# A lookahead of three halves in the first five steps, two transposes two steps later, and three fewer products of zeros

## The chip, the cores and the metric

The kernel runs on one core of a Trainium2 chip. The metric is device time in microseconds (us); lower is better. A time is the median of several executions; the profile is one execution, recorded by the hardware profiler, whose own time is given beside its span. Engines are named as in the profile: PE is TensorE (PEld its weight loads), DVE is VectorE, ACT is ScalarE, POOL is GpSimd and SP is SyncE, which issues most DMAs.

## The reference, cut to what matters

One layer on 256 tokens of width 1024, all in float32: a mixer of two attentions, then a gated feed-forward net with a short convolution, each followed by a residual and a layer norm.

```python
mod = silu(c) @ w_ada + b_ada                      # six rows of 1024: shifts, scales, gates
h = x * (1 + sc1) + sh1
mq, mk, mv, rq, rk, rv, rg, g_a, g_r = split(h @ w_in)
y_a = softmax attention of 8 heads (rotary_half(mq), rotary_half(mk), mv), causal
y_r = retention of 4 heads (retnet_rotate(rq), retnet_rotate(rk), rv); y_r = silu(rg) * head_norm(y_r)
merged = sigmoid(g_a) * (y_a @ w_proj_moba) + sigmoid(g_r) * (y_r @ w_proj_ret)
x = layer_norm(1.189 * x + g1 * (merged @ w_out))
h = x * (1 + sc2) + sh2                            # then the feed-forward net and the second norm
```

`rotary_half` turns each half of a head's q or k against the other: `x1*cos - x2*sin`, `x2*cos + x1*sin`. That is the "rotation" below.

## The kernel before, in words

**Split products.** Every float32 product is made of products of rounded parts. A weight half (a 128x1024 tile, "half" for half of a 1 MB load) is split into `whi`, a rounded copy made by ScalarE (line 1197), and `wlo`, the rest, made by VectorE (line 1211). `mm3` (lines 90 to 93) then makes three TensorE products: high by high, high by low, low by high.

**First phase, up to about 59 us.** It makes the modulation rows and the first columns of `h @ w_in` while their weights arrive (lines 143 to 322). It begins with products of zeros: `fill(n)` (line 160) puts n products of a 128x128 and a 128x512 tile of zeros on TensorE, `PRE` = 4 of them before the eight transposes of line 182 and `POST` = 22 behind them. The first real products are those of line 241, whose high parts come from lines 202 and 221.

**The main loop.** From there on a list `steps` holds one entry per weight half (lines 1246 to 1269 run it). Steps 0 to 3 make rk (load `winB`), 4 to 9 rv (`winV`), 10 to 17 rg, 18 to 33 the gates (`winGr`), 34 to 45 the two projections, and so on. A step of this part is 12 products of 128x512, or from step 18 on 24 of 128x256. Before its products a step prepares (splits) halves ahead: `prep_to(max(need) + 1 + LOOKAHEAD)` with `LOOKAHEAD` = 6, so step s has the halves up to s+6 split in the engines' queues ahead of its own products. There are 8 buffers for split halves and 4 for raw loads; a raw load is issued when the second half of an earlier one has been split. ScalarE's copy of one half more is queued ahead (`ahead`, line 1208). Behind some splits a chained reduction of the modulation rows runs on VectorE (line 174, "ada" in the names).

**The mixers ride along.** `mixers()` (line 955) is a generator that the loop advances three times per step: before the splits, between the splits and the products, and behind the products. Its first part rotates q and k of the two token tiles with eight VectorE operations, at most three per step (lines 919 to 928: two partner products, the product with cos, the sum). `ROT_AT` = 3 says how many steps it rotates before the transposes: behind the products of step 3 `rot_T` transposes q and k of token tile 0 on TensorE (line 934, eight transposes into banks 4 and 5) and ScalarE copies them out (line 936); behind step 4 the same for token tile 1. From the next step on, `i` counts the steps of the attention: `scores` every second step (line 995 on TensorE, line 1001 on VectorE), Exp in the next (line 1027 on ScalarE), its reciprocal (line 1031, VectorE), the scaling (line 1023, ScalarE), four steps behind the scores three transposes per head into bank 5 (line 1038, TensorE) and their copy (line 1040, ScalarE), and the weighted sum of a pair of heads into bank 6 (`attend`, line 1014). In steps 5 to 8 of this count VectorE also rotates q and k of the retention; later come its transposes and the retention itself.

**What is set by the step number and not by `i`.** The sums of rv (line 497) follow steps 6 and 9. The silu of rg follows the products of steps 13 and 17 by one step: it stands in steps 14 and 18, a Sigmoid on ScalarE (line 507) and a product on VectorE (line 508). ScalarE's functions come in tables; where the next function is not in the loaded one, an `ACT_TABLE_LOAD` stands ahead of it.

Engines run their queues in order, so the place of an operation in the program is its place in the queue. The loop's lines that the change touches:

```python
late = LN1_AT < s < LN1_AT + 8
if not late:
    prep_to(max(need) + 1 + (LOOKAHEAD if s < LN1_AT - 1 else HL_BUFS))
run_sides()
```

Of the kernel before, what the change touches and what calls it, by code (L numbers as in the profile page):

```python
# [20 lines left out]
LOOKAHEAD = 6  # L21
RAW_BUFS = 4
HL_BUFS = 8
NG = 4
ROT_AT, RV_AT, RG_AT, LN1_AT = 3, 10, 18, 50


CONST_AT = 1
T0_AT, XN, PRIME = 4, 256, 3
W0, W1, W2 = (4, 5), (6,), (7,)  # L30
PRE, POST = 4, 22


def mixer_ffn(tc, a, out):
    nc = tc.nc
    pe, act, dve, sp = nc.tensor, nc.scalar, nc.vector, nc.sync
    cst = tc.tile_pool(name="cst", bufs=1)
    pools = [cst, tc.tile_pool(name="wts", bufs=1), tc.tile_pool(name="big", bufs=1),
             tc.tile_pool(name="tmp", bufs=2),
             tc.tile_pool(name="ps", bufs=1, space=bass.MemoryType.PSUM),  # L40
             tc.tile_pool(name="dram", bufs=1, space=bass.MemoryType.DRAM)]
    with tc.manual_schedule():
        with pools[0] as cst, pools[1] as wts, pools[2] as big, pools[3] as tmp, pools[4] as ps, \
                pools[5] as dram:
            _body(nc, a, out, pe, act, dve, sp, cst, wts, big, tmp, ps, dram)


def _body(nc, a, out, pe, act, dve, sp, cst, wts, big, tmp, ps, dram):
# [424 lines left out]
    def run_waiting(early):  # L473
        for e in waiting:
            if e[0] <= S["main"] and (not early or e[1]):
                e[2]()
                done_.append(e)
        waiting[:] = [e for e in waiting if e not in done_]
        del done_[:]
# [660 lines left out]
    def residual():  # L1140

        l01, l23 = slot(1, [128, 2, 1024]), slot(11, [128, 2, 1024])
        for i in range(4):
            S["ln", i] = (l01, l23)[i // 2][:, i % 2]
            nc.gpsimd.dma_start(S["ln", i], a["lnrow"][i:i + 1, :].to_broadcast([128, 1024]))
        S["z2"] = [slot(n, [128, 1024]) for n in ("7a", "7b")]
        S["x1"] = S["z1"]
        for _ in range(30):
            yield
        for t in range(2):  # L1150
            for c in range(2):
                z = S["z1"][:, t, c * 512:(c + 1) * 512]
                for i, op in ((0, OP.mult), (1, OP.add)):
                    dve.tensor_tensor(z, z, S["ln", i][:, c * 512:(c + 1) * 512], op)
                    for _ in range(6):
                        yield
# [67 lines left out]
    def prep_to(n, force=False):  # L1224
        while prepped[0] < min(n, 2 * len(main)) and (force or live[0] < HL_BUFS):
            next(pg)
# [14 lines left out]
    def run_sides():  # L1241
        for g in list(sides):
            if next(g, StopIteration) is StopIteration:
                sides.remove(g)

    for s, (need, rel, fn) in enumerate(steps):
        S["main"] = s
        if s == LN1_AT + 8:
            sides.append(residual())
        run_sides()  # L1250
        run_waiting(True)
        prep_to(max(need) + 1, True)
        late = LN1_AT < s < LN1_AT + 8
        if not late:
            prep_to(max(need) + 1 + (LOOKAHEAD if s < LN1_AT - 1 else HL_BUFS))
        run_sides()
        run_waiting(False)
        fn([tiles[h] for h in need])
        for h in rel:
            tiles.pop(h)  # L1260
            live[0] -= 1
        while s % 2 and later and later[0][0] <= s:
            later.pop(0)[1]()
        run_sides()
        if late and s >= LN1_AT + PRIME:
            if s == LN1_AT + PRIME:
                next(pg)
            elif s > LN1_AT + 4:
                prep_to(max(need) + 1 + HL_BUFS)
# [93 lines left out]
```

## Time and profile before

| | |
|---|---|
| median of 3 runs | 436.18 us (435.83 to 437.18) |
| the profiled execution's own time | 436.49 us |
| its span, first to last instruction | 434.7 us |
| TensorE busy | 422.6 us (97%) |
| VectorE busy | 362.5 us (83%) |
| ScalarE busy | 252.2 us (58%) |
| DMA moved | 105.69 MB, mean 243 GB/s |

A row of the timeline has the start in us, the time, the engine, the line, the operation, what it writes and reads, the count of merged instructions, and in brackets the idle time ahead of it on its engine with what ended it. The times of TensorE are starts of products that overlap by a pipeline: 128x512 products that are listed with 0.39 us each start some 0.23 us apart. A row of the waits has who waited, for whom, the total in us, how often, and the longest. The table by stretch has the busy time of each engine in each stretch, then the granted TensorE clock as a share of full speed, the DMA share and GB/s.

### The profile page before, as it was taken

Reading aid. Unit: us, or ns where it says so; the run is one execution under the profiler, and the core shown is the slowest. Engines: PE = TensorE matmul, PEld = TensorE weight load, DVE = VectorE, ACT = ScalarE, POOL = GpSimd, SP = SyncE. Lnnn points to the kernel's source line nnn. Section 1 sums busy time; section 2 is a strip of 40 time slices with the busy share of each in tenths; the row PEclk is TensorE's granted clock in tenths of the full one; section 3 lists DMA queues with packets and bytes.
Section 4 is the critical chain, followed back from the end, with each engine's and each line's share of the span. In section 5 each row is a group of like instructions: output and inputs, shape, how many; then the busy total and the mean of one; then the engine's idle time right before and its main releaser. Section 6 shows DMA issues by size and latency. Waiting matters only on the chain.

```text
span 434.7 us, 6482 instructions
## 1 busy us (share of the span) xinstructions
PE 422.6 (97%) x2466; PEld 366.4 (84%) x2466; DVE 362.5 (83%) x574; ACT 252.2 (58%) x403; POOL 7.3 (2%) x17
## 2 busy tenths in 40 slices
PE   8999998899999999999999999999999999999992
PEld 4888886677779999999988899888888888888882
DVE  4898989779977897887989888899898898678676
ACT  4775577587765575534362898656465466466500
POOL 0000000000000000000000010000000000000000
PEclk9999999899999999999999999999999999999997
DMA  7999989743566689598776059756757768550001
GB/s 245 423 408 376 406 323 361 299 170 123 193 249 239 228 326 350 204 312 322 254 291 262 15 211 388 271 198 201 290 198 284 281 208 331 193 194 0 2 25 72
DMA packets 20447, 105.69 MB, mean 243 GB/s; under 512 B 2608, under 2 KB 4672, under 8 KB 10432
## 3 DMA queue, kind: packets, MB, share of 16 engines
q1 hardware_dynamic: 19008, 100.28, 62.2%
q0 software_dynamic: 1408, 5.01, 3.3%
q8 instruction: 19, 0.31, 0.3%
q14 instruction: 12, 0.10, 0.1%
HBM read 104.22 MB, written 1.06 MB: 242 GB/s over the span
## 4 chain that ended last, share of the span: by engine, by line
PE 80%; DMA 9%; DVE 5%; issue 2%; SPq 1%; ACT 1%; DVEq 0%; ACTq 0%
PE P L91 16%; PE P L92 16%; PE P L93 16%; PE P L102 14%; PE P L100 8%; DMA raw<-in_winB 2%; DMA raw<-in_ada 2%; PE P L99 2%; DMA raw<-in_winX 2%; DMA raw<-in_winA 2%; DMA raw<-in_winV 2%; DVE wlo L228 1%; DVE wlo L1211 1%; SPq L137 1%; PE P L681 1%
## 5 line engine op out<-in xcount | busy, mean ns | idle before, releaser
L1211 DVE TENSOR_TENSOR wlo<-raw,whi 128x1024 fp32r<-128x1024 f32 x120 | 144.9, 1219 | 12.1 <-ACT whi L1197 11.8
L1197 ACT ACTIVATE whi<-raw 128x1024 fp32r<-128x1024 f32 x120 | 125.1, 1054 | 41.1 <-PE P L93 13.5
L93 PE MATMUL P<-whi,A 128*128 128x512 f32 (+1 forms) x156 | 58.6, 376 | 0.0
L102 PE MATMUL P<-AYb,whi 128*128 128x512 f32 x144 | 52.0, 396 | 0.0
L91 PE MATMUL P<-A,whi 128*128 128x256 f32 x160 | 46.0, 288 | 0.0
L93 PE MATMUL P<-A,wlo 128*128 128x256 f32 x160 | 45.3, 283 | 0.0
L92 PE MATMUL P<-A,whi 128*128 128x256 f32 x160 | 45.3, 283 | 0.0
L91 PE MATMUL P<-whi,A 128*128 128x512 f32 (+1 forms) x112 | 43.7, 390 | 0.0
L92 PE MATMUL P<-wlo,A 128*128 128x512 f32 (+1 forms) x112 | 42.5, 379 | 0.0
L174 DVE CUSTOM_DVE_ANT_0 junk<-raw,srow,bcol 128x1024 bf16<-128x1024 f32 x32 | 40.9, 1278 | 0.0
L100 PE MATMUL P<-AYb,wlo 128*128 128x256 f32 x144 | 40.1, 279 | 0.0
L102 PE MATMUL P<-AYa,whi 128*128 128x512 f32 x108 | 39.5, 396 | 0.0
L241 PE MATMUL P<-whi,A 128*128 128x512 f32 x144 | 37.8, 391 | 0.0
L100 PE MATMUL P<-AYa,wlo 128*128 128x256 f32 x144 | 34.3, 279 | 0.0
L93 PEld LDWEIGHTS P<-whi,A 128*128 128x128 f32 x156 | 29.7, 190 | 5.4
L102 PEld LDWEIGHTS P<-AYb,whi 128*128 128x128 f32 x144 | 27.0, 188 | 6.5
L770 DVE SCALAR_TENSOR_TENSOR A<-A,convw 128x255 f32<-128x255 f32 (+1 forms) x44 | 21.3, 483 | 13.3 <-ACT A L766 12.3
L241 PEld LDWEIGHTS P<-whi,A 128*128 128x128 f32 x144 | 27.0, 188 | 5.8
L766 ACT ACTIVATE A<-A,convw 128x256 f32<-128x256 f32 x22 | 13.2, 602 | 30.4 <-DVE A L446 30.3
L91 PEld LDWEIGHTS P<-A,whi 128*128 128x128 f32 x160 | 30.7, 192 | 0.0
L92 PEld LDWEIGHTS P<-A,whi 128*128 128x128 f32 x160 | 30.7, 192 | 0.0
L93 PEld LDWEIGHTS P<-A,wlo 128*128 128x128 f32 x160 | 30.7, 192 | 0.0
(242 smaller groups left out, 873.1 us busy)
## 6 DMA issues: line engine op xcount, KB each, us to landing
raw<-in_ada SPq DMA_DIRECT2D x17, 1024.0 KB, 4.9
raw<-in_wup SPq DMA_DIRECT2D x11, 1024.0 KB, 4.8
raw<-in_wgate SPq DMA_DIRECT2D x11, 1024.0 KB, 5.1
raw<-in_wdown SPq DMA_DIRECT2D x11, 1024.0 KB, 4.8
raw<-in_winGr SPq DMA_DIRECT2D x8, 1024.0 KB, 4.7
raw<-in_winA SPq DMA_DIRECT2D x13, 512.0 KB, 6.7
raw<-in_ada SPq DMA_DIRECT2D x12, 512.0 KB, 8.0
raw<-in_winB SPq DMA_DIRECT2D x6, 1024.0 KB, 6.8
```

What stands on the lines that cost most here:

```text
L91: pe.matmul(o, lh, rh, start=start, stop=False)
L92: pe.matmul(o, lh, rl, start=False, stop=False)
L93: pe.matmul(o, ll, rh, start=False, stop=stop)
L99: pe.matmul(o, wh, x2, start=True, stop=False)
L100: pe.matmul(o[:, :256], wl, x2[:, 0], start=False, stop=False)
L102: pe.matmul(o, wh, x2, start=False, stop=stop)
L174: dve.tensor_tensor_reduce(out=junk[:, rows], in0=raw[:, rows], in1=srow[:, rows] if row is None else row, scale=1.0, scalar=bias(sec, j) ...
L241: pe.matmul(pa[4 * (n == "V") + 2 * c + t], x[:, j, t * 128:(t + 1) * 128], w[:, c * 512:c * 512 + 512], start=first and seen[c] == 1, sto ...
L766: act.activation(g, x, AF.Identity, scale=w(2), bias=w(3))
L770: dve.scalar_tensor_tensor(g[:, 2 - n:], x[:, :254 + n], w(n), g[:, 2 - n:], op0=OP.mult, op1=OP.add)
L1197: act.activation(hi, src, AF.Copy)
L1211: dve.tensor_tensor(lo, src, f(hi), OP.subtract)
```

## The change

Three numbers and a condition. `POST` goes from 22 to 19. `ROT_AT` goes from 3 to 5, so the two `rot_T` stand behind the products of steps 5 and 6, and all that follows in `mixers()` moves two steps later; what is set by the step number stays. In steps 0 to 4 the loop prepares halves up to s+3 (`NEAR`), from step 5 on up to s+6 as before. Line numbers above 25 grow by one.

```diff
-ROT_AT, RV_AT, RG_AT, LN1_AT = 3, 10, 18, 50
+ROT_AT, RV_AT, RG_AT, LN1_AT = 5, 10, 18, 50
+NEAR = 3
...
-PRE, POST = 4, 22
+PRE, POST = 4, 19
...
-            prep_to(max(need) + 1 + (LOOKAHEAD if s < LN1_AT - 1 else HL_BUFS))
+            prep_to(max(need) + 1 + (NEAR if s < ROT_AT else LOOKAHEAD if s < LN1_AT - 1 else HL_BUFS))
```

VectorE's queue from the first rotation operation (step 0) on, before. `A2a` and `A2b` are q and k of token tiles 0 and 1, `A8a` the partner products, `wlo` a split half:

```order
L922 TENSOR_TENSOR A8a<-A2a,sinm 128x16x32
L1211 TENSOR_TENSOR wlo<-raw,whi 128x1024 x5
L922 TENSOR_TENSOR A8a<-A2a,sinm 128x16x32
L927 TENSOR_TENSOR A2a<-A2a,cosm 128x1024
L928 TENSOR_TENSOR A2a<-A2a,A8a 128x1024
L1211 TENSOR_TENSOR wlo<-raw,whi 128x1024
L922 TENSOR_TENSOR A8a<-A2b,sinm 128x16x32 x2
L927 TENSOR_TENSOR A2b<-A2b,cosm 128x1024
L1211 TENSOR_TENSOR wlo<-raw,whi 128x1024
L928 TENSOR_TENSOR A2b<-A2b,A8a 128x1024
L1211 TENSOR_TENSOR wlo<-raw,whi 128x1024 x3
```

The same place after:

```order
L923 TENSOR_TENSOR A8a<-A2a,sinm 128x16x32
L1212 TENSOR_TENSOR wlo<-raw,whi 128x1024 x2
L923 TENSOR_TENSOR A8a<-A2a,sinm 128x16x32
L928 TENSOR_TENSOR A2a<-A2a,cosm 128x1024
L929 TENSOR_TENSOR A2a<-A2a,A8a 128x1024
L1212 TENSOR_TENSOR wlo<-raw,whi 128x1024
L923 TENSOR_TENSOR A8a<-A2b,sinm 128x16x32 x2
L928 TENSOR_TENSOR A2b<-A2b,cosm 128x1024
L1212 TENSOR_TENSOR wlo<-raw,whi 128x1024
L929 TENSOR_TENSOR A2b<-A2b,A8a 128x1024
L1212 TENSOR_TENSOR wlo<-raw,whi 128x1024 x7
```

Two splits instead of five stand between the first and the second rotation operation, and seven instead of three behind the last.

VectorE's queue around the reciprocal of head 6's sums (the `RECIPROCAL` row), before (step 12). `AR` is q or k of the retention, the `L174` rows a chained reduction:

```order
L919 TENSOR_TENSOR A8a<-AR_574,sinr 128x256 x2
L927 TENSOR_TENSOR AR_574<-AR_574,cosr 128x512
L928 TENSOR_TENSOR AR_574<-AR_574,A8a 128x512
L1211 TENSOR_TENSOR wlo<-raw,whi 128x1024
L174 ISA junk,mod<-raw,srow,bcol 128x1024
L174 ISA mod 128x1
L1031 RECIPROCAL mx<-mx 128x2
```

The same place after (step 14):

```order
L920 TENSOR_TENSOR A8a<-AR_571,sinr 128x256 x2
L928 TENSOR_TENSOR AR_571<-AR_571,cosr 128x512
L929 TENSOR_TENSOR AR_571<-AR_571,A8a 128x512
L1212 TENSOR_TENSOR wlo<-raw,whi 128x1024
L175 ISA junk,mod<-raw,srow,bcol 128x1024
L175 ISA mod 128x1
L509 TENSOR_TENSOR A7a<-P_902,A7a 128x512
L509 TENSOR_TENSOR A7b<-P_903,A7b 128x512
L1032 RECIPROCAL mx<-mx 128x2
```

The two products of the first silu now stand ahead of that reciprocal. Two splits higher up in the queue, between the scores of heads 4 and 5 and the rotation that follows them, one chained reduction more has come in as well: before, the first reduction of the loop stood behind that rotation.

ScalarE's queue from head 6's scaling to the copy of head 4's transposes out of bank 5, before (step 13). The number behind `mx` tells the heads apart, `P5` is bank 5:

```order
L1023 ACTIVATE A11_786<-A11_786,mx_1005 128x128
L1023 ACTIVATE A11_786<-A11_786,mx_1005 128x256
L1027 ACTIVATE A11_786,mx_1009<-A11_786,mx_1009 128x128
L1027 ACTIVATE A11_786,mx_1009<-A11_786,mx_1009 128x256
L76 ACTIVATE A5_762<-P6_1081 128x256
L1040 ACTIVATE A9a_1092<-P5_1088 128x384
```

The same place after (step 15), with the silu of step 14 ahead of it:

```order
L508 ACT_TABLE_LOAD
L508 ACTIVATE A7a_1022<-P2_902 128x512
L508 ACTIVATE A7b_1023<-P3_903 128x512
L1041 ACTIVATE A9b_1092<-P5_1088 128x384
L1198 ACTIVATE whi_1099<-raw_968 128x1024
L1024 ACTIVATE A11_821<-A11_821,mx_1044 128x128
L1024 ACTIVATE A11_821<-A11_821,mx_1044 128x256
L1028 ACT_TABLE_LOAD
L1028 ACTIVATE A11_821,mx_1048<-A11_821,mx_1048 128x128
L1028 ACTIVATE A11_821,mx_1048<-A11_821,mx_1048 128x256
L77 ACTIVATE A5_795<-P6_1122 128x256
L1041 ACTIVATE A9a_1133<-P5_1129 128x384
```

The first silu, which stood behind the last Exp, now stands ahead of it, so the table is loaded for the Sigmoid, again for the last Exp and again for the second silu in step 18: two loads more in all.

## The prediction

> **What bounds the kernel now.** I read the waits of TensorE first, since it is the busiest engine.
>
> ```profile
> PE P L934 <- DVE A2b L928: 2.1, 1, 2.1
> PE P L163 <- DVE A10a L157: 1.2, 1, 1.2
> PE P L934 <- DVE A2a L928: 1.0, 1, 1.0
> ```
>
> After its first products it waits only twice in the whole span, both times with the transposes of rotated q and k for VectorE's last rotation operation. The timeline of TensorE around them:
>
> ```profile
> 59.58 0.39 PE L91 MATMUL P<-whi,A 128*128 128x512 f32 x1
> ...
> 70.23 0.39 PE L93 MATMUL P<-whi,A 128*128 128x512 f32 x1
> ...
> 71.64 1.09 PE L934 MATMUL P<-first,A2a 128*128 128x128 f32 x8 [1.02 <-DVE A2a L928]
> ...
> 72.49 0.47 PE L91 MATMUL P<-whi,A 128*128 128x512 f32 x1
> ...
> 75.11 0.39 PE L93 MATMUL P<-whi,A 128*128 128x512 f32 x1
> ...
> 77.61 1.65 PE L934 MATMUL P<-first,A2b 128*128 128x128 f32 x8 [2.10 <-DVE A2b L928]
> ...
> 78.90 0.77 PE L91 MATMUL P<-whi,A 128*128 128x512 f32 x1
> ...
> 81.49 0.39 PE L91 MATMUL P<-whi,A 128*128 128x512 f32 x1
> ```
>
> Steps 0 to 3 are 48 products; from the first (59.58) to the last (70.23) are 47 intervals, 0.227 us each, so a step is 2.72 us. TensorE was free at 70.46 and began to transpose at 71.64: 1.18 us lost. Behind step 4 it was free at 75.34 and began at 77.61: 2.27 us. Then it was slow. The eight transposes took 1.29 us (77.61 to 78.90) where the first eight took 0.85 (71.64 to 72.49), and the six products from 78.90 to 81.49 took 2.59 us where six intervals are 1.36: 0.44 + 1.23 = 1.67 us. The table by stretch has the reason, a granted clock of 0.50 (the column behind POOL's):
>
> ```profile
> 78.00:79.00 1.00, 1.00 (x8) 1.00 (x6) 1.00 (x2) 0.56 (x1) 0.00 (x0) 0.50 0.01 0
> ```
>
> The two waits and their aftermath cost 1.18 + 2.27 + 1.67 = 5.1 us. VectorE's rows say why it was late:
>
> ```profile
> 61.67 2.51 DVE L1211 TENSOR_TENSOR wlo<-raw,whi 128x1024 fp32r<-128x1024 f32 x2
> ...
> 64.80 3.67 DVE L1211 TENSOR_TENSOR wlo<-raw,whi 128x1024 fp32r<-128x1024 f32 x3 [0.62 <-ACT whi L1197]
> 68.39 0.69 DVE L922 TENSOR_TENSOR A8a<-A2a,sinm 128x512 f32<-128x512 f32 x1
> 69.11 1.22 DVE L927 TENSOR_TENSOR A2a<-A2a,cosm 128x1024 f32<-128x1024 f32 x1
> 70.36 1.22 DVE L928 TENSOR_TENSOR A2a<-A2a,A8a 128x1024 f32<-128x1024 f32 x1
> 71.51 1.22 DVE L1211 TENSOR_TENSOR wlo<-raw,whi 128x1024 fp32r<-128x1024 f32 x1
> 72.64 1.29 DVE L922 TENSOR_TENSOR A8a<-A2b,sinm 128x512 f32<-128x512 f32 x2
> ...
> 76.24 1.22 DVE L928 TENSOR_TENSOR A2b<-A2b,A8a 128x1024 f32<-128x1024 f32 x1
> ```
>
> Five splits stand between the first and the second rotation operation, and three of them waited 0.62 us more for a half.
>
> **The rotations and the lookahead of three.** After, the second rotation operation comes at 64.18, behind two splits. From start to start the rows give 0.72 for a partner product, 1.25 for the product with cos, 1.15 for the sum, 1.13 for a split, 1.32 for two partner products. In the new order: A2a is rotated at 64.18 + 0.72 + 1.25 + 1.15 = 67.3; half 4 is split at 68.4; then 1.32 + 1.25 to 71.0, half 5 at 72.1, A2b rotated at 73.3, half 6 at 74.4, half 7 at 75.6, halves 8 to 11 at 80.1. TensorE without waits starts step s at 59.58 + 2.72 s: step 4 at 70.5, step 5 at 73.2, its end at 75.9, transposes to 76.75, step 6 to 79.5, transposes to 80.3. So A2a has 8.6 us of slack and A2b 6.2; half 4 has 2.1, half 5 1.1 and half 6 2.4. The tightest cover is half 5: what VectorE loses beyond 1.1 us by then, TensorE waits. I cost the moved transposes at their 0.85 us as before, and both waits and the slow clock as gone: **-5.1 us**.
>
> What catches up later is halves 8 to 11 in step 5. On ScalarE the copy of half 12 stands ahead of the transposes' copies (line 936), and the load of half 12 is issued only when half 5 is split, at 72.1. Loads land like this:
>
> ```profile
> raw<-in_ada SPq DMA_DIRECT2D x17, 1024.0 KB, 4.9
> ...
> raw<-in_winB SPq DMA_DIRECT2D x6, 1024.0 KB, 6.8
> ```
>
> With 4.9 us (no other load is then in flight) it lands at 77.0. Its copy is at most twice a 128x512 function of 0.60 us (the row at 118.25 below) and two copies of that size follow, so they end by 79.4, just ahead of the second transposes at 79.5, which need those banks. I take 0; with the 6.8 of loads that shared the engines it would be a wait of 1.8 us, the upper bound. POOL's two loads of the decay table move behind the transposes by the same steps; their first reader is the retention, ten steps on.
>
> **What the shift by two steps does to the attention.** The silu of rg stays in step 14 and now falls among the softmax. The rows of before that answer to it, on VectorE, ScalarE and TensorE:
>
> ```profile
> 97.30 0.29 DVE L1001 CUSTOM_DVE_ANT_0 A<-P,mask 128x128 f32<-128x128 f32 x1 [0.41 <-PE P L995]
> ...
> 103.25 1.28 DVE L174 CUSTOM_DVE_ANT_0 junk<-raw,srow,bcol 128x1024 bf16<-128x1024 f32 x1
> ...
> 104.46 0.16 DVE L1031 RECIPROCAL mx<-mx 128x2 f32<-128x2 f32 x1
> ...
> 105.46 0.29 DVE L1001 CUSTOM_DVE_ANT_0 A<-P,mask 128x128 f32<-128x128 f32 x1 [0.48 <-PE P L995]
> ...
> 111.43 0.16 DVE L1031 RECIPROCAL mx<-mx 128x2 f32<-128x2 f32 x1
> ...
> 120.82 0.68 DVE L508 TENSOR_TENSOR A7a<-P,A7a 128x512 f32<-128x512 f32 x1
> ...
> 122.02 1.21 DVE L1211 TENSOR_TENSOR wlo<-raw,whi 128x1024 fp32r<-128x1024 f32 x1
> ```
>
> ```profile
> 111.62 0.80 ACT L1023 ACTIVATE A<-A,mx 128x128 f32<-128x128 f32 x2 [1.44 <-DVE mx L1031]
> ...
> 113.47 0.47 ACT L1040 ACTIVATE A9a<-P 128x384 f32<-128x384 f32 x1
> ...
> 116.96 1.28 ACT L507 ACT_TABLE_LOAD   x1
> 118.25 0.60 ACT L507 ACTIVATE A7a<-P 128x512 f32<-128x512 f32 x1
> ```
>
> ```profile
> 115.37 0.49 PE L1038 MATMUL P<-first,A 128*128 128x128 f32 x3
> ```
>
> Before, the reciprocal of head 6 (111.43) lets ScalarE scale, do the last Exp and then copy head 4's transposes out of bank 5, done at 113.94. Head 5's transposes need that bank at 115.37: a slack of 1.43 us. In this stretch VectorE is behind its own queue, not behind TensorE. After, between the scores of 97.30 and that reciprocal there is one reduction more (103.25 to 104.46: 1.21), of which 0.48 was idle at 105.46, and the two silu products (120.82 to 122.02: 1.20). Then a table load of 1.28 stands ahead of the last Exp. Together 0.73 + 1.20 + 1.28 = 3.21 us, against 1.43 of slack: TensorE waits **+1.8 us** at line 1038 for head 5 (behind step 16). The bounds: 0 if VectorE has caught up by more than the rows say, 3.2 if none of the slack is there. The table load of step 14 I cost at 0: it stands ahead of head 3's copy, which the second weighted sum needs at 111.48 (row below). The scores of 105.46 start at 106.19 after; in the 5.3 us up to that sum must go part of the scores' operations, head 6's Exp (under 1.85, the time from 111.62 to 113.47), the load (1.28) and two silu functions (0.60 each), 4.3 without the first. If that cover went it would be an earlier part of the same wait. The second silu's load, in step 18, stands behind the last scaling and ahead of a copy that is needed a step later.
>
> [...]
>
> One wait goes here, in the chain of waits:
>
> ```profile
> 111.48 0.80 PE P L1014 x8
> ...
> 119.50 1.15 PE P L1014 x7
> ```
>
> The third weighted sum took 1.15 us for 0.80, since its copy stood behind the table load of 116.96; after, none stands between head 5's transposes and their copy: **-0.35 us**.
>
> **Three products of zeros.**
>
> ```profile
> 6.10 3.85 PEld L163 LDWEIGHTS <-A10a 128*128 128x128 bf16 x18 [0.28 <-issue]
> ...
> 8.76 0.60 ACT L202 ACTIVATE A<-AYa,mod 128x256 fp32r<-128x256 f32 x1 [3.10 <-DVE mod L174]
> ...
> 21.86 1.06 ACT L223 ACTIVATE whi<-raw 128x1024 fp32r<-128x1024 f32 x1 [0.47 <-DMA raw<-in_winA]
> ...
> 24.54 0.30 PEld L241 LDWEIGHTS P<-wlo,A 128*128 128x128 f32 x2 [0.38 <-DVE wlo L228]
> ```
>
> They start 3.85 / 18 = 0.21 us apart and end near 10.0; the first real product had its input at 9.36. So three fewer let it start 0.64 us earlier. But at 24.54 TensorE waits for the low part of a weight whose copy on ScalarE had waited for its load at 21.86, whatever TensorE did before: it would only wait 0.64 us longer there. I take **0**, with 0 and -0.64 as bounds. [...]
>
> **Sum.** -5.1 + 1.8 - 0.35 = -3.65, say -3.7. From the profiled execution's 436.49 that is 432.8; its median of runs was 0.31 lower, so I forecast 436.18 - 3.7 = **432.5 us**. Behind step 18 TensorE waits for nothing in the trace up to the end, so what is won stays won.
>
> **Rivals.** *The new wait is hidden*: the gain is 5.1 + 0.35 = 5.4, time 430.8 (430.1 with the products of zeros). For it: lookahead by then lets VectorE's splits slip without harm. Against: the reciprocal is in order behind them. Chance 0.14.
>
> *The clock falls in the new wait.* A gap of 2.27 us halved it, one of 1.18 did not; 1.8 lies between. Price as above 1.67: gain 2.0, time 434.2. Chance 0.14. [...]
>
> *The change doesn't do what it says*: VectorE stays the bound from step 0 to 17 and the waits only move, to the scores and the weighted sums. For it: no idle in its rows from 64.80 on. Against: its last rotation is 6 us early by my sum. About 436. Chance 0.08.
>
> *Slower*: VectorE's lag does not shrink behind step 16, and the transposes of heads 6 and 7 (steps 17 and 18) wait as head 5's do. Three waits of 1.8 are 5.4 us, and with the clock halved behind one of them 7.1, against a gain of 5.4: 1.7 us slower, 437.9. It decides from the point where the waits at line 1038 add up to more than 5.4 us. For it: the reductions go on, one per step. Against: the retention's rotations are over by then, so that a step has a split and a reduction, 1.13 + 1.21 us, for VectorE, against 2.72 us and more for TensorE. Chance 0.06.
>
> **How the numbers follow.** The forecast with its own spread (0.8 to 2.7 us of new wait, 431.6 to 433.5) has 0.58. A measurement of this kernel tells 0.3% (1.3 us) from no change. Faster: 0.58 + 0.14 + 0.14 = 0.86; same 0.08; slower 0.06. The range takes in the hidden wait with part of the zeros at the lower end and the fallen clock at the upper: 430.4 to 434.6; the last two cases, 0.14, lie outside.
>
> **What would show it.** Right: no wait at line 934, full clock from 70 to 85 us, step 7's products ending near 83; VectorE's two silu products ahead of head 6's reciprocal, four table loads in 80 to 130 us where two were, and one TensorE wait of 1 to 2.5 us at line 1039 for ScalarE. Wrong: a wait of TensorE for a split half in steps 4 to 7, a second wait for a copy, or a start of the main loop that has moved from 59.58.

## The result, and the profile after

The change takes 432.60 us (median of 4 runs, 432.49 to 432.80); beside it the kernel before took 436.62 us (4 runs, 435.83 to 437.18). The ratio is 0.991, with a 95% interval of 0.9891 to 0.9929. The forecast was 432.5 us, with a range of 430.4 to 434.6. One execution of the change in the last group of runs took 1079 us: through its whole trace a 128x512 product starts some 0.6 us after the one before, where it is 0.23 in the others, at a listed clock of 1.00; its cause is open, and every ratio leaves it out.

The profiled execution of the change took 432.61 us, with a span of 430.8 us. The waits of TensorE:

```profile
PE P L1039 <- ACT A9a L1041: 1.7, 1, 1.7
PE P L164 <- DVE A10a L158: 1.2, 1, 1.2
PE P L242 <- ACT A L203: 0.4, 1, 0.4
```

The two waits at the transposes of rotated q and k (line 934, now 935) are gone. The first row is the new one, of TensorE for ScalarE at line 1039. The other two lie ahead of the first real products. The same in the timeline of TensorE:

```profile
59.30 0.39 PE L92 MATMUL P<-whi,A 128*128 128x512 f32 x1
...
75.63 1.03 PE L935 MATMUL P<-first,A2a 128*128 128x128 f32 x8
...
79.24 1.04 PE L935 MATMUL P<-first,A2b 128*128 128x128 f32 x8
...
82.97 0.93 PE L996 MATMUL P<-AYb,AYa 64*128 64x128 f32 x8
...
117.29 0.55 PE L1039 MATMUL P<-first,A 128*128 128x128 f32 x3 [1.75 <-ACT A9a L1041]
...
422.78 0.28 PE L94 MATMUL P<-whi,A 128*128 128x256 f32 x1
```

Neither of the two groups of transposes has a bracket, so TensorE came to them without idle time, and step 7 was over at 82.97, where the first scores begin; the prediction said near 83. The first and the last row give a measure that I use below: the *loop length*, from the start of the main loop's first product to the start of the kernel's last. It is 422.78 - 59.30 = 363.48 us. Before, the last product was this one, so that the length was 426.68 - 59.58 = 367.10 us:

```profile
426.68 0.28 PE L93 MATMUL P<-whi,A 128*128 128x256 f32 x1
```

The loop is 3.62 us shorter (forecast: 3.65). The profiled executions differ by 436.49 - 432.61 = 3.88; the other 0.26 is nearly all in the start of the loop, which is 0.28 earlier. VectorE after, with the rotations, then the scores, the chained reduction, the silu products and the reciprocal:

```profile
60.98 2.52 DVE L1212 TENSOR_TENSOR wlo<-raw,whi 128x1024 fp32r<-128x1024 f32 x2
...
65.40 1.23 DVE L929 TENSOR_TENSOR A2a<-A2a,A8a 128x1024 f32<-128x1024 f32 x1
...
70.14 1.22 DVE L1212 TENSOR_TENSOR wlo<-raw,whi 128x1024 fp32r<-128x1024 f32 x1
71.28 1.22 DVE L929 TENSOR_TENSOR A2b<-A2b,A8a 128x1024 f32<-128x1024 f32 x1
72.41 8.03 DVE L1212 TENSOR_TENSOR wlo<-raw,whi 128x1024 fp32r<-128x1024 f32 x7
...
97.32 0.29 DVE L1002 CUSTOM_DVE_ANT_0 A<-P,mask 128x128 f32<-128x128 f32 x1 [1.07 <-PE P L996]
...
99.96 1.28 DVE L175 CUSTOM_DVE_ANT_0 junk<-raw,srow,bcol 128x1024 bf16<-128x1024 f32 x1
...
112.05 0.69 DVE L509 TENSOR_TENSOR A7a<-P,A7a 128x512 f32<-128x512 f32 x1
...
113.25 0.16 DVE L1032 RECIPROCAL mx<-mx 128x2 f32<-128x2 f32 x1
```

Token tile 0 is rotated at 66.63 (65.40 + 1.23) and token tile 1 at 72.50, 9.0 and 6.7 us ahead of their transposes. Half 5 (the row at 70.14) is split at 71.36; step 5 cannot begin before 59.30 + 5 x 2.72 = 72.9. ScalarE after:

```profile
76.11 1.06 ACT L1198 ACTIVATE whi<-raw 128x1024 fp32r<-128x1024 f32 x1 [1.34 <-DMA raw<-in_winB]
...
107.97 1.28 ACT L508 ACT_TABLE_LOAD   x1
...
113.50 0.80 ACT L1024 ACTIVATE A<-A,mx 128x128 f32<-128x128 f32 x2 [1.83 <-DVE mx L1032]
114.31 1.28 ACT L1028 ACT_TABLE_LOAD   x1
115.61 0.40 ACT L1028 ACTIVATE A<-A,mx 128x128 f32<-128x128 f32 x1
...
116.76 0.47 ACT L1041 ACTIVATE A9a<-P 128x384 f32<-128x384 f32 x1
```

The last four rows are the new wait: ScalarE itself waited 1.83 us for the reciprocal, then loaded the table for the last Exp, which began at 115.61, and so came to the copy of bank 5 at 116.76. It was done at 117.23, and TensorE's transposes started at 117.29. From 80 to 130 us there are four table loads (84.16, 107.97, 114.31, 125.27) where before has two, as forecast. The table by stretch shows what became of the clock, first where the kernel before had half the clock, then behind the new wait:

```profile
78.00:79.00 1.00, 1.00 (x6) 0.82 (x5) 1.00 (x2) 1.00 (x2) 0.00 (x0) 1.00 1.02 418
...
117.00:118.00 1.00, 0.71 (x7) 0.71 (x7) 0.99 (x3) 1.00 (x2) 0.00 (x0) 1.00 0.56 66
118.00:119.00 1.00, 1.00 (x9) 0.93 (x8) 0.94 (x2) 1.00 (x4) 0.00 (x0) 1.00 0.50 197
```

It is 1.00 in all three, as in every stretch of 1 us from the start of the loop to 428 us. And in the chain of waits, which lists one of the eight products less for before, the third weighted sum takes 0.80 us where it took 1.15:

```profile
121.46 0.80 PE P L1015 x8
```

### The profile page after: what moved, and what is told of

Read it like the earlier page. It is cut to its first block, busy times and chain, and to the rows that moved or that the text cites. A ratio compares the mean times of both kernels' runs of the same rounds, so it can differ in the third digit from the quotient of the medians.

```text
span 430.8 us, 6476 instructions
## 1 busy us (share of the span) xinstructions
PE 419.6 (97%) x2463; PEld 364.3 (85%) x2463; DVE 362.9 (84%) x574; ACT 255.0 (59%) x405; POOL 7.3 (2%) x17
## 4 chain that ended last, share of the span: by engine, by line
PE 91%; DVE 5%; DMA 1%; ACT 1%; SPq 0%; issue 0%; DVEq 0%; ACTq 0%
PE P L92 16%; PE P L94 16%; PE P L93 16%; PE P L103 14%; PE P L242 12%; PE P L101 8%; PE P L100 2%; DMA raw<-in_ada 1%; DVE junk L175 1%; PE P L682 1%; PE P L685 1%; PE P L684 1%; PE P L935 1%; DVE wlo L1212 1%; PE P L996 1%; DVE A L1002 1%
```

## The experiments

The theory is the forecast's own sum: the two rotation waits and the half clock go (-5.1), a wait at line 1039 comes (+1.8), which is made of VectorE's queue and a table load, the third weighted sum gets 0.35 shorter, and the products of zeros do nothing. The rivals: the gain comes from the products of zeros; the new wait has another cause, the extra table load alone. Since a time and its start vary by more than some of these terms (below), each kernel is also read by its loop length.

| kernel | loop, from to (us) | length | time, median (us) | ratio to before, 95% |
|---|---|---|---|---|
| before | 59.58, 426.68 | 367.10 | 436.62 | |
| the change | 59.30, 422.78 | 363.48 | 432.60 | 0.9910 (0.9891 to 0.9929) |
| POST = 19 alone | 61.80, 427.77 | 365.97 | 436.71 | 1.0027 (0.9994 to 1.0060) |
| ROT_AT = 5 alone | 60.95, 424.44 | 363.49 | 433.43 | 0.9951 (0.9927 to 0.9976) |
| lookahead alone | 59.41, 421.38 | 361.97 | 432.26 | 0.9917 (0.9887 to 0.9947) |
| the change, ROT_AT = 4 | 59.39, 422.68 | 363.29 | 432.77 | 0.9933 (0.9912 to 0.9955) |
| the change, first silu in step 16 | 59.69, 421.22 | 361.53 | 431.16 | 0.9897 (0.9858 to 0.9935) |
| the change, silu's products in step 16 | 61.32, 423.73 | 362.41 | 431.87 | 0.9905 (0.9873 to 0.9937) |
| the change, silu's products twice | 61.85, 428.35 | 366.50 | 436.68 | 1.0022 (0.9996 to 1.0047) |
| lookahead alone, first silu in step 15 | 61.00, 422.62 | 361.62 | 431.75 | 0.9905 (0.9872 to 0.9939) |

The time of before in the first row is that beside the change. The four kernels after the change stood against a before of 435.12 us (27 runs), the last four against one of 436.37 us (21 runs). Each length is of one profiled execution.

**The products of zeros alone.**

```diff
-PRE, POST = 4, 22
+PRE, POST = 4, 19
```

> Only POST = 19; the rest as before. My theory: the time does not change (within 0.3 us), since TensorE gives the 0.64 us back at products whose low parts of the weights come late; the two waits at the transposes stay at 1.0 and 2.1 us. Rival: part of the earlier start is kept. In the profile of the change the main loop's first product starts 0.28 us earlier than before (59.30 for 59.58); if the fills are the reason, it starts at 59.30 here too, and, as the waits at the transposes are set by VectorE, the time still moves by less than 0.3 us.

The waits of TensorE, and the stretch behind the second:

```profile
PE P L934 <- DVE A2b L928: 2.1, 1, 2.1
PE P L934 <- DVE A2a L928: 1.5, 1, 1.5
...
81.00:82.00 1.00, 1.00 (x8) 0.87 (x7) 1.00 (x2) 1.00 (x3) 0.34 (x1) 1.00 0.00 0
```

Both waits are still there. The ratio is 1.0027 (0.9994 to 1.0060); the 0.64 us that the prediction gave as a bound would be 0.9985, below the interval. So these products bring nothing that can be measured, and the rival falls. What I had not expected is the clock: after the same wait, of 2.12 us by the timeline, it stayed at 1.00, in this stretch and in all others up to the last product. The loop is 1.13 us shorter than before for that reason: -1.67 for the clock and +0.48 for the first wait (1.50 for 1.02) are -1.19.

**The shift by two steps alone.**

```diff
-ROT_AT, RV_AT, RG_AT, LN1_AT = 3, 10, 18, 50
+ROT_AT, RV_AT, RG_AT, LN1_AT = 5, 10, 18, 50
```

> Only ROT_AT = 5, with the lookahead of six halves and 22 fills as before. Theory A, the shift alone removes the waits: q and k of tile 0 are rotated at 71.6 and of tile 1 at 77.5 as before, TensorE wants them at 75.9 and 79.5, so no wait at the transposes, and the new wait for head 5's transposes of 1.75 us as in the change: 3.7 us faster than before. Theory B, the short lookahead is needed: a wait of over 0.5 us is left at the transposes and the gain is under 3 us.

The first row of the waits of TensorE:

```profile
PE P L1038 <- ACT A9a L1040: 1.7, 1, 1.7
```

No wait at the rotations, and the new wait as in the change. The loop length, 363.49 us, is the change's to 0.01. So the shift alone already does all that the change does, and the new wait belongs to the shift.

**The lookahead alone** (three halves in the first five steps, transposes where they were).

```diff
-            prep_to(max(need) + 1 + (LOOKAHEAD if s < LN1_AT - 1 else HL_BUFS))
+            prep_to(max(need) + 1 + (3 if s < 5 else LOOKAHEAD if s < LN1_AT - 1 else HL_BUFS))
```

> Only the lookahead of three halves in steps 0 to 4; the transposes stay behind steps 3 and 4, 22 fills. Theory A: the lookahead alone removes both waits (tile 0 rotated at 67.3 for 70.5, tile 1 at 73.3 for 74.0), and as the attention is not moved there are no further table loads and no wait for head 5's transposes: 5.1 us faster than before, 1.4 us faster than the change; the wait of 0.35 us at the third weighted sum stays. Rival: the four splits that are made up in step 5 now stand ahead of the scores of heads 0 and 1 on VectorE, and TensorE waits 1 to 2 us for the attention later: a gain of 3 to 4 us.

TensorE has no wait in the main loop at all. The loop length is 361.97 us, 5.13 less than before, where the prediction put the two waits and the half clock at 1.18 + 2.27 + 1.67 = 5.12. In its chain of waits the third weighted sum still takes 1.15 us, so that this kernel has the first term of the sum and no other:

```profile
114.19 1.15 PE P L1014 x7
```

The lookahead alone beats the whole change by 1.5 us of loop length, because it removes the same waits and brings no new one. The times of the two come from different groups of runs; this verdict rests on the loop lengths.

**The change with the shift of one step.**

```diff
-ROT_AT, RV_AT, RG_AT, LN1_AT = 5, 10, 18, 50
+ROT_AT, RV_AT, RG_AT, LN1_AT = 4, 10, 18, 50
```

> The change with ROT_AT = 4 instead of 5 (lookahead of three in steps 0 to 3, 19 fills). The first silu then follows the last Exp within step 14, so there are two table loads as before, not four. If the new wait comes from the extra table load ahead of the last Exp alone, it is gone: no TensorE wait at line 1039, 1.75 us faster than the change. If it is the sum of the queues, head 4's copy out of bank 5 ends at 113.94 plus 0.73 (one reduction more) plus 1.28 (the silu's table load) plus 1.0 (its two functions) = 116.95, and TensorE waits 1.5 us: the same as the change within 0.3 us.

The lookahead of three ends with `ROT_AT`, so here it holds for steps 0 to 3.

ScalarE around the copy, and the waits of TensorE:

```profile
110.70 0.49 ACT L1028 ACTIVATE A<-A,mx 128x256 f32<-128x256 f32 x1
...
111.31 1.28 ACT L508 ACT_TABLE_LOAD   x1
...
113.84 0.51 ACT L1041 ACTIVATE A9a<-P 128x384 f32<-128x384 f32 x1
```

```profile
PE P L1039 <- ACT A9a L1041: 1.5, 1, 1.5
```

The last Exp now stands ahead of the silu, so there are two table loads in the stretch, as before the change, not four. TensorE still waits 1.5 us, since the load for the Sigmoid and the two functions behind it (111.31 to 113.84) stand ahead of the copy. So the wait does not need the extra table loads; what is queued ahead of that copy makes it.

**The change with the first silu two steps later** (in step 16, behind the last Exp).

```diff
-            put_off(1, silu)
+            put_off(1 if cc else 3, silu)
```

> The change, with the first silu put off from step 14 to step 16 (behind the last scaling, so two table loads as before, and its products behind head 6's reciprocal). Theory (the new wait is the sum of one reduction, two silu products and one table load, 3.21 us, less 1.43 us of slack): only the reduction's 0.73 us is left, inside the slack, so TensorE does not wait at line 1039. From the main loop's first product to the last product of the kernel the change takes 363.5 us; here 361.7 us. Rival (the reductions alone, which the shift brought forward, make VectorE late): a wait of over 0.7 us stays.

ScalarE from head 6's scaling to the copy:

```profile
112.63 0.80 ACT L1024 ACTIVATE A<-A,mx 128x128 f32<-128x128 f32 x2 [2.03 <-DVE mx L1032]
113.34 0.39 ACT L1028 ACTIVATE A<-A,mx 128x128 f32<-128x128 f32 x1
...
114.48 0.47 ACT L1041 ACTIVATE A9a<-P 128x384 f32<-128x384 f32 x1
```

The transposes on TensorE that this copy lets go:

```profile
115.78 0.49 PE L1039 MATMUL P<-first,A 128*128 128x128 f32 x3
```

No load stands in between, the copy begins 1.85 us behind the scaling where it was 3.26 (113.50 to 116.76), and the wait is gone. So a load in that place costs 1.41 us, of which 1.28 is its row. The copy ends at 114.95, 0.83 us ahead of the transposes, where before it was 1.43: the one reduction more, which this kernel still has, costs 0.60 of the slack (the forecast's sum has 0.73). The loop is 1.95 us shorter than the change's, for a wait of 1.75.

**Only silu's VectorE products later.** The two Sigmoids stay in step 14.

```diff
                     act.activation(o, bk[t], AF.Sigmoid)
+                put_off(0 if cc else 2, product)
+            def product():
+                for t in range(2):
+                    o = S["rg"][t][:, cc * 512:(cc + 1) * 512]
                     dve.tensor_tensor(o, bk[t], o, OP.mult)
```

> The change, with only the two products of the first silu on VectorE put off to step 16; its Sigmoid and both table loads stay in steps 14 and 15. Theory (sum of the queues): 1.20 us less ahead of head 6's reciprocal, so the wait at line 1039 falls from 1.75 to 0.55 us, and main loop to last product from 363.5 to 362.3 us. Rival (the table load alone decides, ScalarE is late whatever VectorE does): the wait stays at 1.75 us.

In the waits of TensorE:

```profile
PE P L1043 <- ACT A9a L1045: 0.5, 1, 0.5
```

With the table loads left and VectorE's 1.20 us taken out of the reciprocal's way, 0.5 us are left (forecast: 0.55; 0.46 by the timeline). So 1.29 us of the wait go with the two products on VectorE (1.20 us in the rows of before). What is left is the reduction and the load less the slack: by the two figures of the kernel ahead 0.60 + 1.41 - 1.43 = 0.58. No run takes the reduction away by itself.

**Those products made twice.** A second one stands behind each of the two; the second ones write a part of the tile that a later step overwrites.

```diff
                     dve.tensor_tensor(o, bk[t], o, OP.mult)
+                    if cc == 0:
+                        dve.tensor_tensor(S["rg"][t][:, 512:1024], bk[t], o, OP.mult)
```

> The change, with the two products of the first silu made twice on VectorE (1.20 us more ahead of head 6's reciprocal; the second pair goes to columns that are written again later). Theory: the wait at line 1039 grows by all of it, 1.75 to 2.95 us, and main loop to last product from 363.5 to 364.7 us if the granted clock stays at full. The clock: if a gap of over 2.1 us always halves it, it falls here and the stretch is 1.7 us longer still, 366.4 us; if the fall depends on where the gap lies in time, the runs split into two groups some 1.7 us apart.

VectorE from the first of the four products to the reciprocal, the timeline of TensorE at the wait, and the stretches behind it:

```profile
114.60 0.69 DVE L509 TENSOR_TENSOR A7a<-P,A7a 128x512 f32<-128x512 f32 x1
...
117.25 0.15 DVE L1034 RECIPROCAL mx<-mx 128x2 f32<-128x2 f32 x1
```

```profile
121.28 0.55 PE L1041 MATMUL P<-first,A 128*128 128x128 f32 x3 [3.19 <-ACT A9a L1043]
```

```profile
122.00:123.00 1.00, 1.00 (x9) 0.91 (x8) 0.95 (x2) 1.00 (x4) 0.00 (x0) 0.79 0.73 238
123.00:124.00 1.00, 1.00 (x4) 0.80 (x3) 1.00 (x2) 1.00 (x3) 0.00 (x0) 0.50 0.95 401
124.00:125.00 1.00, 1.00 (x3) 0.78 (x3) 1.00 (x2) 1.00 (x2) 0.00 (x0) 0.50 0.81 344
125.00:126.00 1.00, 1.00 (x4) 0.73 (x3) 1.00 (x2) 0.16 (x1) 0.00 (x0) 0.51 0.01 0
```

The four products hold up the reciprocal for 2.65 us (114.60 to 117.25) where the two held it up for 1.20 (112.05 to 113.25). These 1.45 us more make the wait 1.44 us longer (3.19 for 1.75; the expected 2.95 had counted 1.20), and now the clock falls to 0.50. The loop grows by 3.02 us: 1.44 of wait, and 1.58 that I put down to the clock (the price in the kernel before was 1.67). This kernel is as slow as the one before the change: the price of the prediction's fallen-clock rival was real, only not at 1.75 us.

**The lookahead alone, with the first silu one step later.**

```diff
-            put_off(1, silu)
+            put_off(1 if cc else 2, silu)
-            prep_to(max(need) + 1 + (LOOKAHEAD if s < LN1_AT - 1 else HL_BUFS))
+            prep_to(max(need) + 1 + (3 if s < 5 else LOOKAHEAD if s < LN1_AT - 1 else HL_BUFS))
```

> Before, with the lookahead of three halves in steps 0 to 4 alone (transposes behind steps 3 and 4, 22 fills), and the first silu put off by one step, to step 15. The lookahead alone took 362.0 us from the main loop's first to the last product. Theory: the table load no longer stands ahead of head 5's copy, so the third weighted sum takes 0.80 us for 1.15: 361.6 us, 1.9 us less than the change. Rival: the load then delays head 6's copy and its transposes' successors instead: 362.0 us or more.

TensorE has no wait in the main loop. The chain of waits has the third weighted sum at

```profile
115.77 0.80 PE P L1014 x8
```

and the loop length is 361.62 us: 0.35 less than with the lookahead alone. That is the third term of the sum by itself, as large as forecast.

**The change and the two best kernels side by side**, on another chip: the change, the change with the silu in step 16, and the lookahead with the silu in step 15, as above.

> The change once more, beside the two versions below on one chip. From the main loop's first to the last product 363.5 us, of which 1.7 to 1.8 us are the wait at line 1039; the kernel's time some 3.6 us below before where before pays for the half clock, some 2 us where it does not.

> The change with the first silu in step 16, once more: main loop to last product 361.5 us and a time 1.9 us (0.4%) below the change, if the first phase, which varies by up to 2.5 us from run to run whatever the kernel, comes out alike over the rounds. Rival: the difference is lost in that variation, under 0.5 us.

> Before with the lookahead of three alone and the first silu in step 15, once more: main loop to last product 361.6 us and a time 1.9 us below the change, equal to the version with the silu in step 16 within 0.5 us: the move of the transposes by two steps is then not needed. Rival: its rotations have under 1 us of slack at the transposes behind step 4, and in some runs it waits there: 0.5 to 2 us slower than the other version.

The kernel before took 435.50 us (11 runs). The change: 433.00 us, ratio 0.9945 (0.9928 to 0.9963). This group has no trace of it that can be set beside the others, so its wait was not seen a second time. Silu in step 16: 431.09 us, 0.9903 (0.9886 to 0.9919). Lookahead with silu in step 15: 431.26 us, 0.9907 (0.9890 to 0.9925). Both beat the change by 1.7 to 1.9 us, and their intervals lie below its own; between themselves they cannot be told apart, as their loop lengths in this group (361.53 and 361.63 us) say too. So the version to keep is the small one: a lookahead of three in five steps and one silu put off by a step, with no shift. It has little to spare, though. Token tile 1 must be rotated ahead of the second transposes; in the first trace of this kernel that is just so:

```profile
74.06 1.22 DVE L928 TENSOR_TENSOR A2b<-A2b,A8a 128x1024 f32<-128x1024 f32 x1
```

```profile
75.50 1.03 PE L934 MATMUL P<-first,A2b 128*128 128x128 f32 x8
```

That is a slack of 75.50 - 75.28 = 0.22 us. In its second trace it is 1.47 us and with the lookahead alone 1.53; the change has 6.7. The rival of slack under 1 us thus came in one trace of three, but none of them has a wait there.

## Why the prediction was right

*Both rotation waits and the half clock, -5.1.* Right as a sum: the lookahead alone measures -5.13. The reason given, splits queued ahead of the rotation on VectorE, is shown by the same kernel, which changes nothing else. The sum was over-covered, since either half of the edit does it alone.

*No wait for halves 4 to 7.* Right. Half 5, named as the tightest, was split 1.5 us before it was needed (forecast: 1.1). The copy of half 12 started at 76.11, where its load was expected to land at 77.0, and nothing waited behind it.

*The new wait, +1.8 for head 5.* Right in place, size and make: 1.75 us at line 1039. The runs support the sum of three queue terms less the slack (0.73 + 1.20 + 1.28 - 1.43): without the two products on VectorE 0.5 is left (forecast 0.55), without these and the loads nothing, and with the products twice 3.19. That the sum fits to 0.05 us is in part luck: the reduction cost 0.60 for 0.73 and the load 1.41 for 1.28, and the two errors cancel. The table load of step 14, costed at 0, was right too: head 3's copy begins at 110.23, and the second weighted sum, which needs it, starts at 111.43 without a wait. In the trace the last Exp starts 1.30 us behind the start of its load (114.31 to 115.61), for 1.28 in the sum.

*Third weighted sum, -0.35.* Right: 1.15 to 0.80, and 0.35 of loop length where it is the only difference.

*Products of zeros, 0.* Right, by the kernel that has them alone. The start of the loop moved from 59.58 to 59.30 in the change, which the prediction had named as a sign against it. The runs show no effect of the edit in it: with 22 such products the loop of the profiled executions started at 59.41 to 61.00 us, with 19 at 59.30 to 61.85.

*The clock.* Here the prediction was right by the median but not in its reading. It took the 1.67 us as a fixed price of a wait of 2.27 us ("A gap of 2.27 us halved it, one of 1.18 did not"), and it is one that only some executions pay. Each run lists its mean granted clock. An execution that spends some 3.4 us at half clock in the loop (3.42 in the profile of before, 3.40 with the products twice) loses 3.4 x 0.5 / 435 = 0.004 of that mean, and the 59 runs of the kernel before that stood beside the experiments fall in two groups with nothing in between: 28 of 59 at 0.989 to 0.991, with a median of 436.52 us, and 31 at 0.993 to 0.997, with one of 434.89. The difference is 1.63 us, near the 1.67 of the rows. The two profiled executions that were read above fit: 0.990 with the half clock in the rows (before), 0.995 without it (POST = 19 alone). So the change is worth 3.65 us by the sum against an execution of the first group and 3.65 - 1.67 = 2.0 against one of the second; the medians, with 432.78 us for the nine runs of the change, say 3.7 and 2.1. That fits a ratio of 0.991 in one group of runs and of 0.9945 in another, where 4 of 11 runs of before had the lower clock: both are right for their mix. Of the first group's four runs of before the clock is on record for one, which had the lower. On the chip of the other group alone, the change's 432.95 us (five runs) is 3.0 below the runs of before with the lower clock and 1.5 below the rest, in the same order but less than the sums. The forecast time hardly hangs on it (434.89 - 2.0 = 432.9), but the forecast gain does: taken from one profiled execution, it took over that execution's luck.

The rivals: a hidden wait (430.8) and a change that doesn't do what it says fell with the first trace, as did waits for heads 6 and 7, for which TensorE has no row. The fallen clock in the new wait (434.2) did not come in any run of the change; the last section has what the runs show of it.

## What to carry to other kernels

When an engine that works in order is late for one product, count what stands in its queue ahead of the operation that is waited for: here a smaller lookahead, which only reorders the queue, removed the same waits as moving the consumer by two steps (the loop got 5.13 us shorter), and it brought no new wait elsewhere. When a consumer is moved and other work keeps its step number, write down who is now ahead of whom on every engine, and add up the queue: a sum of three rows less a slack gave the new wait. And before a stall's after-effect is put into a forecast, see in how many runs it occurs.

## What the runs showed of the hardware that was not expected

Whether TensorE's clock halves after a wait differs from execution to execution, and the share of executions grows with the wait. Counted by the mean granted clock of each run (0.992 and below is the lower clock), for the longest wait inside the main loop:

| longest wait (us, profiled execution) | kernels | runs | with the lower clock |
|---|---|---|---|
| none to 0.5 | lookahead alone, silu later (two kernels, twice each), products later | 41 | 0 |
| 1.5 to 1.75 | the change (twice), ROT_AT = 5 alone, ROT_AT = 4 | 30 | 0 |
| 2.1 | before; POST = 19 alone | 71 | 33 |
| 3.2 | silu's products twice | 12 | 11 |

The mean is a rough sign, since it also holds the half clock behind the kernel's last product, which was 2.7 us in the profile of the change and 5.2 in that of before. With the products twice, six of the 11 are at 0.992, as is the profiled execution, whose rows show the fall.

The traces say more than the count. The stretches in which the clock of before changes, in the loop and behind the last product, and the one behind the last product of the change:

```profile
77.00:78.00 1.00, 0.39 (x4) 0.42 (x5) 1.00 (x2) 0.00 (x0) 0.00 (x0) 0.96 0.89 369
81.00:82.00 1.00, 1.00 (x5) 0.77 (x5) 0.00 (x0) 0.00 (x0) 0.00 (x0) 0.83 1.05 442
429.00:430.00 1.00, 0.00 (x0) 0.00 (x0) 1.00 (x4) 0.00 (x0) 0.00 (x0) 0.75 0.00 0
```

```profile
428.00:429.00 1.00, 0.00 (x0) 0.00 (x0) 0.00 (x0) 0.00 (x0) 0.00 (x0) 0.55 0.70 251
```

The stretches between a fall and a rise show 0.50 and the rest 1.00, so I read a mean of 0.96 as half clock for 0.08 us. So before fell at 77.92, rose at 81.34 and fell again at 429.50, and the change fell at 428.10; with the products twice, by the rows from 122 to 126 us above, the clock fell at 122.58 and rose at 125.98. In the loop the half clock lasted 3.42 us in before and 3.40 us with the products twice. Four waits compare like this:

| kernel | wait, from to (us) | length (us) | clock behind it |
|---|---|---|---|
| before | 75.51 to 77.61 | 2.10 | 0.50 from 77.92 to 81.34 |
| POST = 19 alone | 78.18 to 80.30 | 2.12 | 1.00 |
| the change | 115.54 to 117.29 | 1.75 | 1.00 |
| silu's products twice | 118.09 to 121.28 | 3.19 | 0.50 from 122.58 to 125.98 |

In these four traces the clock halved 0.31 us behind the end of a wait of 2.10 us and 1.30 us behind the end of one of 3.19, and stayed at 1.00 behind waits of 1.75 and 2.12. So at some 2.1 us the length of the wait alone does not say whether the clock falls, and in the count it did in 33 of 71 runs. What else decides it is not shown, and no wait between 1.75 and 2.1 us was tried.
